# Eight modulation columns moved from the tensor engine to the vector engine, and the softmax's division from the vector engine to the scalar engine

## The chip, the core and the metric

The kernel runs on one core of one Trainium2 chip. A core has engines that run side by side, each through its own list of instructions in order: TensorE (PE in the rows; PEld is its weight load), VectorE (DVE), ScalarE (ACT), GpSimd (POOL) and SyncE (SP), which here issues transfers. The metric is the device time of one execution in microseconds (us), as the median of several runs.

## What is computed

A two-layer backbone of a diffusion generator: 256 latent tokens and 256 context tokens of width 1024. Layer 0 mixes tokens by windowed attention with sink logits and by a two-way gated recurrence (HGRN2), side by side; layer 1 by a two-way retention; each layer ends with a SwiGLU feed-forward. Each sub-layer is modulated by vectors that come from a matrix product of the conditioning with `mod_w`: six chunks of 1024 for each layer (shift, scale and gate, twice), for two streams (latent and context).

```python
m_lat = jnp.split((cond_lat @ mod_w[layer] + mod_b[layer])[:, None, :], 6, axis=-1)
m_ctx = jnp.split((cond_ctx @ mod_w[layer] + mod_b[layer])[None, None, :], 6, axis=-1)
...
s_lat = jnp.where(valid, s_lat, -jnp.inf)
s_ctx = jnp.einsum('bkgqd,bkcd->bkgqc', qb, k_ctx, preferred_element_type=F32) * scale
p = jax.nn.softmax(jnp.concatenate([sink_col, s_lat, s_ctx], axis=-1), axis=-1)
...
x = x + m_lat[2] * y_lat
x = x + m_lat[5] * swiglu(modulate(rms_norm(x, norm_g[layer, 1]), m_lat[3], m_lat[4]), ...)
```

## The kernel before

Activations lie with features on the 128 partitions and tokens along the free axis (latent tokens first, then context). All large products take their weights in fp32 as two parts: `ensure` loads a block of 8 tiles of 128x128 (`raw`), ScalarE rounds it to `whi` (L268), VectorE subtracts to get `wlo` (L269), two blocks ahead of use, and `mm3` (L336 to L338) issues three matmuls for each product. These matmuls set the pace of the program text: `work` counts the columns they stream and calls `tick` every 1600 columns. A tick calls `mod_tick` and then moves one step on in each of several lanes (generators): the attention lane, two HGRN lanes, a lane of norms. The order on each engine is then made by a scheduler that takes priorities from this text; it also sets which instruction of a lane stands before which weight split.

The attention lane works on 24 score blocks of 128 queries (8 heads, 3 blocks each). `softmax_scores` makes a block: two matmuls into a bank of PSUM, on VectorE the maximum (L640, L641), on ScalarE the exponential with its sum (L644) and the sink's term (L646), on VectorE the sum's reciprocal (L647, L648) and the division of the probabilities (L650): one instruction of 512 columns for a latent block, two of 256 columns for a pair of context blocks. Five ticks later `softmax_T` transposes the block on TensorE (L656) and ScalarE copies the result out (L658); `attn_pv` multiplies by the values (L675), and its result is split by L416 and L417. The HGRN lanes have some 30 instructions of VectorE for each of 4 heads (L715 to L816), the lane of norms those of L873 to L880.

The modulation is cut into 80 tasks of 128 output features. Layer 0's chunks 0 and 1 are made ahead of everything by TensorE (`mod0a`, L175). For the rest, `mod_tick` starts tasks at a given number of ticks, in the order of `ORD`, and `mod_until` makes up for those that are missing where a chunk is needed. `mod_load` fetches a task's 128x1024 weights (`mr`, three buffers) up to three tasks ahead. `mod_one` does a task with one multiply-and-sum on VectorE for each stream (L233: an instruction of 1024 columns that leaves its sum in an accumulator, and a read of the accumulator). Chunk 3 of layer 0 (the one in `PES`) goes another way, two tasks at a time, by `mod_pe`: 8 matmuls with the conditioning as the 32-column stationary operand (L206), a copy to SBUF on ScalarE (L209), 2 small matmuls that add up the groups (L212), and a small addition on VectorE (L154). A matmul with plain fp32 operands shows as two records in the trace. Four such pieces stand in the program, and all of chunk 3 falls into the first mixer.

Of the kernel before, what the change touches and what calls it, by code (L numbers as in the profile page):

```python
# [37 lines left out]
FA = 2  # L38
PES = [3]
ORD = [2, 3, 4, 5]  # L40
# [28 lines left out]
def hybrid_kernel(ctx, tc, xT, wst, mw0, mwT, small, cbc, cst, imask, dmat, out, order):  # L69
# [128 lines left out]

    def mod_pe(i):

        l, ch, k = mod_tasks[i]
        ps = axb()
        for j in range(2):
            t = mod_load(i + j)[:].rearrange("p (g n) -> p g n", g=4)
            for g in range(4):
                T.matmul(ps[32 * g:32 * g + 32, 0:L], cT[:, 4 * j + g, :], t[:, g, :], start=(j == 0), stop=(j == 1),  # L206
                         skip_group_check=True)
        part = u()[:, 0:L]
        A.activation(part, ps[:, 0:L], AF.Copy)  # L209
        ps2 = ps[:, L:L + 4].rearrange("p (c s) -> p c s", s=2)  # L210
        for c in range(2):
            T.matmul(ps2[:, c, :], part[:, c * P:(c + 1) * P], sel, start=True, stop=True, skip_group_check=True)  # L212
        mod_finish(l, ch, k, k + 2, ps2.rearrange("p c s -> p s c"))

    def mod_step():
        l, ch, k = mod_tasks[min(mod_pos[0], len(mod_tasks) - 1)]
        return 2 if l == 0 and ch in PES else 1

    def mod_one():
        i = mod_pos[0]  # L220
        n = mod_step()
        mod_pos[0] += n
        if n == 2:
            return mod_pe(i)
        l, ch, k = mod_tasks[i]
        mr = mod_load(i)
        streams = (0, 1) if (l == 0 or ch < 2) else (0,)
        for s in streams:
            if s == streams[-1]:
                o = mr[:]  # L230
            else:
                o = u((P, D), BF16)[:]
            V.tensor_tensor_reduce(o, mr[:], cb[:, s, :], 1.0, 0.0, ALU.mult, ALU.add, mvec(l, s, ch, k))  # L233
        if k == KD - 1:
            mod_finish(l, ch)
# [9 lines left out]
    def mod_tick():  # L245
        tickn[0] += 1
        if tickn[0] >= modt[0] * mod_step():
            tickn[0] -= modt[0] * mod_step()
            if mod_pos[0] < len(mod_tasks):
                mod_one()  # L250
# [368 lines left out]
    def softmax_scores(t, j, which):  # L619
# [29 lines left out]
        for i in range(nq):  # L649
            V.tensor_scalar(p[:, i * w:(i + 1) * w], p[:, i * w:(i + 1) * w], den[:, i:i + 1], None, ALU.mult)  # L650
        return p
# [667 lines left out]
```

## Time and profile before

| | |
|---|---|
| median of 3 runs (lowest to highest) | 1146.19 us (1146.14 to 1147.27) |
| the profiled execution's own time | 1146.45 us |
| its span, first to last instruction | 1144.6 us |
| busy share of the span: TensorE, VectorE, ScalarE | 98%, 67%, 48% |
| share of the span's chain that ended last: TensorE, VectorE, ScalarE, DMA | 84%, 10%, 3%, 1% |

The profiled execution lies 0.26 us above the median; 1.85 us of it lie outside the span. The share of the chain tells which engine's work was the last to end before the next step could start, followed back from the end. A busy share is an average over stages: TensorE's matmuls overlap in the pipeline, so that the engine can read as busy while it loses a few tenths of a microsecond; what it did is better read from when each instruction starts.

### The profile page before, as it was taken

What the parts mean: (1) busy time and instruction counts of PE and PEld (TensorE: products, weight loads), DVE (VectorE), ACT (ScalarE), POOL (GpSimd) and SP (SyncE); (2) the same over time, 40 slices, a digit from 0 to 9 for tenths busy, and PEclk for the clock granted to TensorE, in tenths of its full rate; (3) what the DMA queues carried; (4) which work ended last, traced back from release to release, by engine and by line L of the source; (5) the groups of instructions that cost most, each with busy time, mean ns of one, the idle gap of its engine ahead of it and who ended that gap; (6) DMA issues with size and microseconds to landing.
All of it is one profiled execution on the core that took longest, in us unless ns stands there. A gap on an engine that the chain in (4) does not pass through costs nothing.

```text
span 1144.6 us, 18866 instructions
## 1 busy us (share of the span) xinstructions
PE 1116.4 (98%) x7514; PEld 996.9 (87%) x7514; DVE 767.4 (67%) x1399; ACT 554.0 (48%) x948; POOL 20.8 (2%) x46
## 2 busy tenths in 40 slices
PE   3999999999999999999999998999999999999998
PEld 1777877888998888988888898999999999999998
DVE  3877698899798557357883678374646577555553
ACT  5676676664753231123322476454445657544441
POOL 0012000000000000000000000000000000000000
PEclk9999999999999999999999999999999999999999
DMA  9987221326237446247983324343434265655553
GB/s 329 349 235 184 92 65 66 112 74 202 94 113 241 143 147 202 77 139 237 324 308 109 95 75 129 111 131 109 148 94 147 92 203 167 192 183 181 184 183 109
DMA packets 56121, 182.46 MB, mean 159 GB/s; under 512 B 6368, under 2 KB 9824, under 8 KB 55904
## 3 DMA queue, kind: packets, MB, share of 16 engines
q1 hardware_dynamic: 53648, 176.45, 47.6%
q0 software_dynamic: 2240, 4.72, 1.7%
q8 instruction: 59, 0.97, 0.4%
q14 instruction: 30, 0.25, 0.1%
q10 hardware_dynamic: 144, 0.08, 0.0%
HBM read 177.56 MB, written 1.05 MB: 156 GB/s over the span
## 4 chain that ended last, share of the span: by engine, by line
PE 84%; DVE 10%; ACT 3%; DMA 1%; issue 1%; DVEq 0%; ACTq 0%; SPq 0%
PE mm L338 23%; PE mm L337 23%; PE mm L336 23%; PE ax L337 2%; PE ax L336 2%; PE ax L338 2%; DVE wlo L269 2%; DMA raw<-in_wst_dram 1%; PE ax L175 1%; PE ax L656 1%; ACT whi L268 1%; PE ax L675 1%; DVE u L459 1%; PE mm L411 1%; PE mm L409 1%
## 5 line engine op out<-in xcount | busy, mean ns | idle before, releaser
L268 ACT ACTIVATE whi<-raw 128x1024 fp32r<-128x1024 f32 x230 | 243.3, 1059 | 403.0 <-PE mm L337 242.9
L269 DVE TENSOR_TENSOR wlo<-raw,whi 128x1024 fp32r<-128x1024 f32 x230 | 280.7, 1222 | 166.5 <-ACT whi L268 165.9
L336 PE MATMUL mm<-hh,whi 128*128 128x256 f32 (+1 forms) x1072 | 362.2, 339 | 1.2 <-ACT whi L268 0.9
L338 PE MATMUL mm<-hh,wlo 128*128 128x256 f32 (+1 forms) x1072 | 361.6, 338 | 0.6 <-DVE wlo L269 0.6
L337 PE MATMUL mm<-hl,whi 128*128 128x256 f32 (+1 forms) x1072 | 362.0, 338 | 0.1
L337 PE MATMUL mm<-u,whi 128*128 128x256 f32 (+2 forms) x768 | 236.9, 309 | 0.0
L338 PE MATMUL mm<-u,wlo 128*128 128x256 f32 (+2 forms) x768 | 236.7, 308 | 0.0
L336 PE MATMUL mm<-u,whi 128*128 128x256 f32 (+2 forms) x768 | 236.3, 308 | 0.3 <-DVE x L483 0.3
L338 PEld LDWEIGHTS mm<-hh,wlo 128*128 128x128 f32 x1072 | 204.4, 191 | 21.8 <-DVE wlo L269 0.8
L336 PEld LDWEIGHTS mm<-hh,whi 128*128 128x128 f32 x1072 | 204.2, 191 | 21.9 <-ACT whi L268 0.9
L337 PEld LDWEIGHTS mm<-hl,whi 128*128 128x128 f32 x1072 | 204.3, 191 | 20.2 <-DVE hl L466 0.3
L336 PEld LDWEIGHTS mm<-u,whi 128*128 128x128 f32 x768 | 146.4, 191 | 7.9 <-issue 0.4
L338 PEld LDWEIGHTS mm<-u,wlo 128*128 128x128 f32 x768 | 146.6, 191 | 7.2
L337 PEld LDWEIGHTS mm<-u,whi 128*128 128x128 f32 x768 | 146.6, 191 | 7.1
L233 DVE CUSTOM_DVE_ANT_0 mr<-mr,cb 128x1024 f32<-128x1024 f32 x72 | 87.1, 1222 | 13.2 <-DMA mr<-in_mwT_dram 12.6
L416 ACT ACTIVATE u<-u 128x512 fp32r<-128x512 f32 (+1 forms) x84 | 43.0, 526 | 36.7 <-DVE u L1007 17.3
L1007 DVE TENSOR_TENSOR u<-u,mm 128x512 f32<-128x512 f32 (+1 forms) x40 | 22.1, 553 | 44.7 <-PE mm L338 44.7
L233 DVE CUSTOM_DVE_ANT_0 u<-mr,cb 128x1024 bf16<-128x1024 f32 x40 | 48.4, 1219 | 2.8 <-DMA mr<-in_mwT_dram 1.5
L417 DVE TENSOR_TENSOR u<-u,u 128x512 fp32r<-128x512 f32 (+1 forms) x84 | 46.5, 565 | 5.0 <-ACT u L416 4.9
L336 PE MATMUL ax<-u,u 128*128 128x256 f32 x160 | 45.9, 287 | 3.1 <-ACT u L416 3.1
L483 DVE SCALAR_TENSOR_TENSOR x<-mm,modv,x 128x256 f32<-128x256 f32 x48 | 22.4, 480 | 36.1 <-PE mm L338 36.1
L337 PE MATMUL ax<-u,u 128*128 128x256 f32 x160 | 46.0, 287 | 0.0
(220 smaller groups left out, 1216.4 us busy)
## 6 DMA issues: line engine op xcount, KB each, us to landing
raw<-in_wst_dram SPq DMA_DIRECT2D x230, 512.0 KB, 3.8
mr<-in_mwT_dram SPq DMA_DIRECT2D x80, 512.0 KB, 4.5
u<-in_mw_dram SPq DMA_DIRECT2D x16, 256.0 KB, 5.2
u<-u POOLq DMA_DIRECT2D x20, 128.0 KB, 5.7
u<-in_dmat_dram POOLq DMA_DIRECT2D x8, 256.0 KB, 3.0
raw<-in_mw_dram SPq DMA_DIRECT2D x6, 256.0 KB, 5.2
mr<-in_mw_dram SPq DMA_DIRECT2D x6, 256.0 KB, 5.2
x<-in_xT_dram SPq DMA_DIRECT2D x8, 128.0 KB, 3.4
```

What stands on the lines that cost most here:

```text
L175: T.matmul(ps[32 * g:32 * g + 32, :], cT[:, k, :], mws[nt * 8 + k], start=(k < 4), stop=(k >= 4), skip_group_check=True)
L233: V.tensor_tensor_reduce(o, mr[:], cb[:, s, :], 1.0, 0.0, ALU.mult, ALU.add, mvec(l, s, ch, k))
L268: A.activation(hi[:], src[:], AF.Copy)
L269: V.tensor_tensor(lo[:], src[:], hi[:].bitcast(F32), ALU.subtract)
L336: T.matmul(o, w[0], a[0], start=first, stop=False, skip_group_check=shared)
L337: T.matmul(o, w[0], a[1], start=False, stop=False, skip_group_check=shared)
L338: anchor[0] = T.matmul(o, w[1], a[0], start=False, stop=last, skip_group_check=shared)
L409: T.matmul(ps[t][:], a[0], w[0], start=(k == 0), stop=False)
L416: A.activation(hi, src, AF.Copy)
L417: V.tensor_tensor(lo, src, hi.bitcast(F32), ALU.subtract)
L483: V.scalar_tensor_tensor(xs(m, s), ps[:, sl], mvec(l, s, ch, m), xs(m, s), ALU.mult, ALU.add)
L1007: V.tensor_tensor(g[:, 0:w], g[:, 0:w], ps[2 * i + 1][:, 0:w], ALU.mult)
```

## The change

Chunk 3 of layer 0 is made like all others, and the division in the softmax goes to ScalarE, as a copy with the reciprocal as its scale. `mod_pe` and `mod_step` go; the task counter moves on by one task at each due tick, where a piece of chunk 3 took two tasks at twice the interval. The host lays out the weights of chunk 3 like the rest.

```diff
@@ hybrid_kernel
-    def mod_pe(i):
-
-        l, ch, k = mod_tasks[i]
-        ps = axb()
-        for j in range(2):
-            t = mod_load(i + j)[:].rearrange("p (g n) -> p g n", g=4)
-            for g in range(4):
-                T.matmul(ps[32 * g:32 * g + 32, 0:L], cT[:, 4 * j + g, :], t[:, g, :], start=(j == 0), stop=(j == 1),
-                         skip_group_check=True)
-        part = u()[:, 0:L]
-        A.activation(part, ps[:, 0:L], AF.Copy)
-        ps2 = ps[:, L:L + 4].rearrange("p (c s) -> p c s", s=2)
-        for c in range(2):
-            T.matmul(ps2[:, c, :], part[:, c * P:(c + 1) * P], sel, start=True, stop=True, skip_group_check=True)
-        mod_finish(l, ch, k, k + 2, ps2.rearrange("p c s -> p s c"))
...
     def mod_one():
         i = mod_pos[0]
-        n = mod_step()
-        mod_pos[0] += n
-        if n == 2:
-            return mod_pe(i)
+        mod_pos[0] += 1
         l, ch, k = mod_tasks[i]
...
-        if tickn[0] >= modt[0] * mod_step():
-            tickn[0] -= modt[0] * mod_step()
+        if tickn[0] >= modt[0]:
+            tickn[0] -= modt[0]
...
@@ softmax_scores
         for i in range(nq):
-            V.tensor_scalar(p[:, i * w:(i + 1) * w], p[:, i * w:(i + 1) * w], den[:, i:i + 1], None, ALU.mult)
+            A.activation(p[:, i * w:(i + 1) * w], p[:, i * w:(i + 1) * w], AF.Copy, scale=den[:, i:i + 1])
```

The scheduler makes a new order from this. It differs on TensorE, VectorE, ScalarE and SyncE within layer 0's first mixer alone; from the last heads' norms on, and so through both feed-forwards and all of layer 1, every engine has the same instructions in the same order. Line numbers of the changed kernel are 24 lower behind `mod_pe` (L209 there is the multiply-and-sum, L245 the split, L616 to L626 the softmax, L626 its division).

VectorE, where the attention lane has its first blocks (before, 97.8 to 103.7 us). Before (L593 and L632 prepare queries and scores, L154 ends the first piece of `mod_pe`):

```order
L593 TENSOR_TENSOR u_896<-u_757,u_894 128x512
L632 TENSOR_TENSOR ax_978<-ax_978,u_110 128x128
L640 TENSOR_REDUCE s_982<-ax_978 128x1
L647 TENSOR_TENSOR s_939<-s_939,s_940 128x1
L641 TENSOR_SCALAR s_982<-s_982,nsk 128x1
L648 RECIPROCAL s_939<-s_939 128x1
L650 TENSOR_SCALAR u_943<-u_943,s_939 128x512
L154 TENSOR_TENSOR modv<-ax_960,sml 128x2x2
L269 TENSOR_TENSOR wlo_1065<-raw_1062,whi_1064 128x1024
```

Now, at the same place:

```order
L569 TENSOR_TENSOR u_896<-u_757,u_894 128x512
L608 TENSOR_TENSOR ax_970<-ax_970,u_110 128x128
L209 ISA u_915,modv<-mr_794,cb 128x1024
...
L616 TENSOR_REDUCE s_974<-ax_970 128x1
L209 ISA mr_794,modv<-mr_794,cb 128x1024
...
L623 TENSOR_TENSOR s_944<-s_944,s_945 128x1
L209 ISA u_967,modv<-mr_841,cb 128x1024
...
L624 RECIPROCAL s_944<-s_944 128x1
L617 TENSOR_SCALAR s_974<-s_974,nsk 128x1
L209 ISA mr_841,modv<-mr_841,cb 128x1024
...
L608 TENSOR_TENSOR ax_1028<-ax_1028,u_110 128x128
L245 TENSOR_TENSOR wlo_1057<-raw_1054,whi_1056 128x1024
```

Two tasks stand here, four multiply-and-sums (the reads of the accumulator behind each are left out), between the steps of two softmax blocks and ahead of the split; the division is gone. The other six tasks stand alone, two instructions each: two more before 145 us of the old trace, three between 145 and 205 us, one at some 211 us.

VectorE, where the first HGRN head's second direction begins (before, 150.1 to 153.5 us; L718 is a scan, L720 and L723 use it). Before:

```order
L718 SCALAR_TENSOR_TENSOR u_1520<-u_111,u_1422 128x512
L640 TENSOR_REDUCE s_1548<-ax_1544 128x1
L647 TENSOR_TENSOR s_1507<-s_1507,s_1508 128x2
L720 TENSOR_TENSOR u_1422<-u_1520 128x512
L648 RECIPROCAL s_1507<-s_1507 128x2
L723 TENSOR_TENSOR ex_1523<-u_1520 128x8
L641 TENSOR_SCALAR s_1548<-s_1548,nsk 128x1
L650 TENSOR_SCALAR u_1511<-u_1511,s_1507 128x256 x2
L632 TENSOR_TENSOR ax_1575<-ax_1575,u_110 128x128
L269 TENSOR_TENSOR wlo_1765<-raw_1762,whi_1764 128x1024
```

Now:

```order
L694 SCALAR_TENSOR_TENSOR u_1504<-u_111,u_1406 128x512
L209 ISA u_1523,modv<-mr_1121,cb 128x1024
...
L623 TENSOR_TENSOR s_1491<-s_1491,s_1492 128x2
L696 TENSOR_TENSOR u_1406<-u_1504 128x512
L624 RECIPROCAL s_1491<-s_1491 128x2
L699 TENSOR_TENSOR ex_1507<-u_1504 128x8
L209 ISA mr_1121,modv<-mr_1121,cb 128x1024
...
L616 TENSOR_REDUCE s_1537<-ax_1533 128x1
L608 TENSOR_TENSOR ax_1564<-ax_1564,u_110 128x128
L617 TENSOR_SCALAR s_1537<-s_1537,nsk 128x1
L245 TENSOR_TENSOR wlo_1944<-raw_1941,whi_1943 128x1024
```

One task of two multiply-and-sums stands between the scan and the maximum of the next score block, and the two half divisions are gone.

ScalarE at the same place. Before (L725, L726 and L724 are small exponentials of the HGRN lane, L803 a copy out of PSUM):

```order
L725 ACTIVATE ex_1523<-u_1520 128x8
L726 ACTIVATE ex_1523<-u_1520 128x8
L724 ACTIVATE ex_1523<-ex_1523 128x8
L644 ACTIVATE u_1553,s_1549<-ax_1544,s_1548 128x512
L646 ACTIVATE s_1550<-s_1548,sml 128x1
L658 ACTIVATE u_1573<-ax_1568 128x512
L644 ACTIVATE u_1584,s_1580<-ax_1575,s_1579 128x512
L646 ACTIVATE s_1581<-s_1579,sml 128x1
```

Now:

```order
L701 ACTIVATE ex_1507<-u_1504 128x8
L702 ACTIVATE ex_1507<-u_1504 128x8
L626 ACTIVATE u_1495<-u_1495,s_1491 128x256 x2
L700 ACTIVATE ex_1507<-ex_1507 128x8
L620 ACTIVATE u_1542,s_1538<-ax_1533,s_1537 128x512
L622 ACTIVATE s_1539<-s_1537,sml 128x1
```

The division (L626) stands in ScalarE's list ahead of the next block's exponential, and it waits for the reciprocal (L624) of VectorE's list.

## Rows read from the trace of the kernel before

**Rows 1.** The page's first part: each engine's busy time over the whole span, its share and its number of instructions.

```profile
PE 1116.4 (98%) x7514; PEld 996.9 (87%) x7514; DVE 767.4 (67%) x1399; ACT 554.0 (48%) x948; POOL 20.8 (2%) x46
```

**Rows 2.** The page's second part: busy tenths of TensorE and VectorE in 40 slices of 28.6 us each (slices 4 to 10 hold the first mixer).

```profile
PE   3999999999999999999999998999999999999998
DVE  3877698899798557357883678374646577555553
```

**Rows 3.** The chain that ended last, in order of time, some pieces of it: start in us, length in us, what.

```profile
145.10 0.48 DVE u L650
...
174.55 0.28 ACT u L209
174.87 0.61 PE ax L212 x4
...
232.90 0.68 DVE u L720
...
266.66 1.15 DVE wlo L269
267.87 4.38 DMA raw<-in_wst_dram
```

**Rows 4.** Busy time of each engine in three stretches of the first mixer: stretch, its length, then busy us and (in brackets) instructions of PE, PEld, DVE, ACT and POOL, the granted clock, the share of the DMA engines and GB/s.

```profile
95.00:145.00 50.00, 50.00 (x312) 40.73 (x311) 35.65 (x102) 34.95 (x86) 5.61 (x11) 1.00 0.50 137
145.00:205.00 60.00, 59.36 (x550) 47.36 (x552) 53.77 (x142) 43.60 (x105) 2.28 (x6) 1.00 0.22 72
205.00:277.00 72.00, 71.52 (x564) 59.32 (x556) 68.97 (x142) 42.00 (x90) 1.98 (x5) 1.00 0.37 115
```

**Rows 5.** TensorE in order of time around the first and the third piece of `mod_pe`: start us, us, engine, line, operation, out<-in, shapes, count, and in brackets the idle time before.

```profile
96.13 1.07 PE L206 MATMUL ax<-mr,cT 128*32 128x256 f32 x16
97.13 0.50 PE L626 MATMUL ax<-u,u 128*128 128x512 f32 x1
...
102.79 0.50 PE L212 MATMUL ax<-con,u 128*128 128x2 f32 x4
103.15 0.49 PE L411 MATMUL mm<-whi,hl 128*128 128x512 f32 x1
...
174.04 0.39 PE L336 MATMUL mm<-hh,whi 128*128 128x512 f32 x1
174.87 0.61 PE L212 MATMUL ax<-con,u 128*128 128x2 f32 x4 [0.44 <-ACT u L209]
```

**Rows 6.** Groups of instructions by line and shape, of `mod_pe`'s matmuls on TensorE and its copy on ScalarE: out<-in, shapes, count | busy us, mean ns of one | idle us before them and what ended most of it.

```profile
L206 PE MATMUL ax<-mr,cT 128*32 128x256 f32 x64 | 4.3, 385 | 0.0
L212 PE MATMUL ax<-con,u 128*128 128x2 f32 x16 | 2.2, 243 | 0.4 <-ACT u L209 0.4
L209 ACT ACTIVATE u<-ax 128x256 f32<-128x256 f32 x4 | 1.5, 375 | 1.4 <-PE ax L206 1.4
```

**Rows 7.** VectorE in order of time: two places with the division of the softmax (L650) and the instruction after it, and two multiply-and-sums (L233) in a row.

```profile
145.10 0.48 DVE L650 TENSOR_SCALAR u<-u,s 128x512 f32<-128x512 f32 x1
145.49 1.22 DVE L269 TENSOR_TENSOR wlo<-raw,whi 128x1024 fp32r<-128x1024 f32 x1
...
177.99 0.61 DVE L650 TENSOR_SCALAR u<-u,s 128x256 f32<-128x256 f32 x2
178.52 0.34 DVE L816 SCALAR_TENSOR_TENSOR u<-u,ex,ax 128x128 f32<-128x128 f32 x1
...
264.29 1.22 DVE L233 CUSTOM_DVE_ANT_0 mr<-mr,cb 128x1024 f32<-128x1024 f32 x1
265.44 1.22 DVE L233 CUSTOM_DVE_ANT_0 u<-mr,cb 128x1024 bf16<-128x1024 f32 x1
```

**Rows 8.** The busy time of L650 alone on VectorE in the first two stretches, with the number of instructions.

```profile
95.00:145.00 50.00, 6.79 (x17) 1.00 0.50 137
145.00:205.00 60.00, 5.81 (x15) 1.00 0.22 72
```

**Rows 9.** Groups of instructions on ScalarE by line and shape, as in rows 6: the nearest to a scaled copy in SBUF.

```profile
L416 ACT ACTIVATE u<-u 128x512 fp32r<-128x512 f32 x46 | 29.0, 630 | 36.3 <-DVE u L1007 17.3 <-DVE u L1109 7.8 <-DVE u L880 4.9
L416 ACT ACTIVATE u<-u 128x256 fp32r<-128x256 f32 x38 | 14.0, 401 | 0.5 <-DVE u L1159 0.5
L432 ACT ACTIVATE u<-x,gsv 128x256 fp32r<-128x256 f32 x24 | 11.9, 494 | 0.0
L644 ACT ACTIVATE u<-ax,s 128x512 f32<-128x512 f32 x16 | 11.0, 687 | 7.6 <-DVE s L641 7.3 <-issue 0.3
```

**Rows 10.** What VectorE waited for in the second and in the third stretch, the longest of each: line, released by, us in total, times, longest.

```profile
DVE s L647 <- ACT s L646: 1.8, 2, 1.2
...
DVE u L715 <- ACT u L294: 2.0, 2, 1.5
```

**Rows 11.** Where TensorE starts right behind another engine: ScalarE's copy of transposes and the matmuls after it, and transposes that wait for VectorE.

```profile
149.06 0.58 ACT L658 ACTIVATE u<-ax 128x512 f32<-128x512 f32 x1
...
149.71 0.64 PE L656 MATMUL ax<-con,u 128*128 128x128 f32 x4
...
277.16 0.72 PE L878 MATMUL ax<-con,u 128*128 128x128 f32 x3 [0.43 <-DVE u L873]
```

**Rows 12.** What the multiply-and-sum L233 waited for in the whole run (us, times), and a wait of SyncE's queue of transfers between 90 and 280 us (us in total, times, longest).

```profile
  DMA mr<-in_mwT_dram: 14.0, 17
...
SPq L196 <- PE ax L206: 18.0, 4, 5.0
```

More of the change, by code (lines that the diff above doesn't have):

```diff
@@ L38 @@
 FA = 2
-PES = [3]
 ORD = [2, 3, 4, 5]
@@ L197, in mod_load @@
         return mod_raw[i]
-    def mod_pe(i):
-        l, ch, k = mod_tasks[i]
-        ps = axb()
-        for j in range(2):
-            t = mod_load(i + j)[:].rearrange("p (g n) -> p g n", g=4)
-            for g in range(4):
-                T.matmul(ps[32 * g:32 * g + 32, 0:L], cT[:, 4 * j + g, :], t[:, g, :], start=(j == 0), stop=(j == 1),
-                         skip_group_check=True)
-        part = u()[:, 0:L]
-        A.activation(part, ps[:, 0:L], AF.Copy)
-        ps2 = ps[:, L:L + 4].rearrange("p (c s) -> p c s", s=2)
-        for c in range(2):
-            T.matmul(ps2[:, c, :], part[:, c * P:(c + 1) * P], sel, start=True, stop=True, skip_group_check=True)
-        mod_finish(l, ch, k, k + 2, ps2.rearrange("p c s -> p s c"))
-    def mod_step():
-        l, ch, k = mod_tasks[min(mod_pos[0], len(mod_tasks) - 1)]
-        return 2 if l == 0 and ch in PES else 1
     def mod_one():
         i = mod_pos[0]
-        n = mod_step()
-        mod_pos[0] += n
-        if n == 2:
-            return mod_pe(i)
+        mod_pos[0] += 1
         l, ch, k = mod_tasks[i]
@@ L1270 @@
     for i, ch in enumerate(ORD):
-        cols = slice(ch * D, (ch + 1) * D)
-        if ch in PES:
-            t = mw[0][:, cols].reshape(2, 4, P, 4, 256).transpose(3, 0, 2, 1, 4)
-        else:
-            t = mw[0][:, cols].T
-        mt[8 * i:8 * i + 8] = t.reshape(8, P, D)
+        mt[8 * i:8 * i + 8] = mw[0][:, ch * D:(ch + 1) * D].T.reshape(8, P, D)
     ew = I['even_w_in'][0]
```

## The prediction

> **What bounds the kernel now.** I read the shares first: TensorE is busy 98% of the span, VectorE 67%, ScalarE less than half [rows 1]. An average can hide stages, so the slices come next: TensorE shows 9 nearly everywhere, and VectorE is at 8 or 9 in slices 6 to 11 (143 to 315 us), where the first mixer runs [rows 2]. The change touches only that mixer, so the rest of the span, which is TensorE's, can be set aside.
>
> Inside the mixer I cut three stretches at the places where the chain changes hands: 95 to 145, 145 to 205 and 205 to 277 us. TensorE is busy in all of them (50.00 of 50, 59.36 of 60, 71.52 of 72), at a granted clock of 1.00. VectorE has 35.65 of 50 us in the first, 53.77 of 60 in the second, 68.97 of 72 in the third; ScalarE 34.95, 43.60 and 42.00 [rows 4]. So in the first stretch VectorE has 14.3 us to spare, in the second 6.2, in the third 3.0. The chain says the same in another way: it runs through VectorE from 145.10 us on, with the division itself as its first step, comes back to TensorE at 174.87 us, and is VectorE's again from 232.90 to 267.8 us [rows 3]. The reader should see two engines that are both nearly full: taking work from TensorE helps only as far as VectorE keeps up, and the change loads VectorE.
>
> How close they run is seen where TensorE starts: ScalarE's copy at 149.06 us lasts 0.58 and ends at 149.64; the transposes behind it start at 149.71. At 277.16 us TensorE has waited 0.43 us for VectorE's L873 [rows 11]. There is almost no slack, but hardly any loss either.
>
> **The change, part by part.** *TensorE loses the four pieces.* The 16 records of L206 take 1.00 us from their start to that of the next instruction (96.13 to 97.13), L212 0.36 us (102.79 to 103.15) [rows 5]; by the groups a piece's L212 is busy 2.2/4 = 0.55 us [rows 6]. I take 1.45 us for a piece. The third piece also made TensorE wait: a matmul that is normally followed after 0.23 us was followed after 0.83 (174.04 to 174.87), behind the copy L209 [rows 5], which is 0.60 us more. Two pieces lie in the first stretch, the third in the second; the fourth begins at the border and is counted in the third. Sum: 2.9, 2.05 and 1.45, in all 6.4 us.
>
> *VectorE gains sixteen multiply-and-sums and loses the divisions.* One L233 follows the other after 1.15 us (264.29, 265.44) [rows 7]: 16 x 1.15 = 18.4 us. A division of 512 columns frees the engine after 0.39 us, a pair of 256 after 0.53 [rows 7]. The first stretch holds 17 instructions, which are 9 single ones and 4 pairs, the second 15, which are 7 and 4 pairs [rows 8]: 5.6 and 4.9 us. From the order shown above, eight multiply-and-sums come into the first stretch, six into the second, two into the third. So VectorE's work changes by 9.2 - 5.6 = +3.6 us, 6.9 - 4.9 = +2.0 and +2.3. The three small additions that go with `mod_pe` I put at nothing in sum (some 0.1 us each, against the one larger addition at the end of the chunk).
>
> *ScalarE gains the divisions and loses four copies.* A scaled copy in SBUF with a pointer for the scale is not there at 512 columns. A plain one takes 630 ns, the exponential with pointers 687; at 256 columns a plain one takes 401, a scaled one 494 [rows 9]. Instructions overlap by some 0.1 us on this engine, so that I take 0.6 and 0.4 us; the bounds are 0.5/0.3 and 0.7/0.5. First stretch 9 x 0.6 + 8 x 0.4 = 8.6, second 7.4, less 0.375 for each copy L209 [rows 6]. ScalarE goes to some 42.8 us in the first stretch and 50.6 in the second: of the time that TensorE would leave (47.1 and 57.95) that is 91% and 87%.
>
> VectorE does the same division faster, in 0.39 us to the 0.6 taken here for 512 columns [rows 7, 9]. The Trainium skill (ScalarE: Activation LUTs, Rules for kernel authors) says for multiplications to use VectorE rather than ScalarE. It speaks against this half of the change, and the two rows agree with it in price; the sum by either is the same, since the page prices the instruction and not the queue, but a kernel in which ScalarE then fills up is the second rival below.
>
> *Transfers* cost nothing in the sum: the same 80 loads of modulation weights are issued, three tasks ahead. L233 has waited for them 14.0 us in all, and SyncE has waited 18.0 us for L206 to free buffers [rows 12]; now VectorE frees them. Behind such a load stand weight loads in the same queue. What hides them is the distance of two blocks; if that is used up, a load costs the 4.38 us of [rows 3].
>
> *The new wait.* ScalarE's division waits for VectorE's reciprocal, and behind it on ScalarE stand the next exponential, the copies of transposes and the rounding of weights, for which TensorE and VectorE wait in turn. Before, one engine did reciprocal and division without asking. And each L233 holds VectorE for 1.15 us ahead of a maximum or a reciprocal.
>
> **The sum by stretches.** First: TensorE sets the pace and VectorE's 3.6 us fit into its 14.3. It would be -2.9 us. ScalarE at 91% will cost some of it; I give back 0.6 (bounds: nothing, and all of 2.9): -2.3. Second and third: VectorE's work is 53.77 + 2.0 = 55.8 and 68.97 + 2.3 = 71.3 us, and the stretch lasts that plus what VectorE still idles. It idled 6.2 and 3.0 us, partly for TensorE's pace, partly for ScalarE (L647 for the sink's exponential 1.8 us, L715 for the gates' logarithm 2.0) [rows 10]. The first kind goes when VectorE runs behind, the second stays; bounds are none and all. I take half: 3.1 and 1.5 us. That gives 58.9 and 72.8 us, -1.1 and +0.8. TensorE alone would need 57.95 and 70.55, so VectorE sets both. After 277 us all orders are as before: nothing. Sum: -2.3 - 1.1 + 0.8 = -2.6 us. On the profiled execution's 1146.45 us that is 1143.85, on the median, 0.26 lower, 1143.6.
>
> In one formula, with i for the idle time that is left to VectorE between 145 and 277 us: change = i - 7.2 us. It was 9.2 us, and I take 4.6.
>
> **Rivals.** *TensorE keeps the pace.* If VectorE and ScalarE fill their gaps nearly without loss (i under 2.4), the floor is TensorE's own: -4.8 to -6.4 us, 1139.8 to 1141.4. For it: the scheduler has moved the weight splits ahead of the tasks. Against: VectorE would be at 98% over 130 us in order, with two partners.
>
> *ScalarE takes the pace in the softmax.* Full to 91% on average in the first stretch, it has bursts: if these hold up TensorE's transposes, the first stretch gives back all of its 2.9 us, and the second its 2.05, while the third keeps about its +0.8: 1146 to 1147, no change that counts. For it: TensorE starts 0.07 us behind ScalarE's copies already [rows 11]. Against: five ticks lie between a block's scores and its transposes.
>
> *Slower: VectorE's idle time does not shrink.* Its place is 145 to 277 us, the mechanism the multiply-and-sums that stand in order ahead of what ScalarE and TensorE wait for: VectorE is late with a reciprocal, ScalarE with the division and all behind it, and VectorE then waits for ScalarE's sums (L647) as long as before. With i = 9.2 the second and third stretch are 2.0 and 2.3 us longer; with half of the first stretch's gain given back it is +2.8 us, 1149.0. It decides from i = 7.2 on, that is, if more than three quarters of the old idle time stay.
>
> A result of no effect at all is not among them: the order shows that the instructions move.
>
> **Numbers.** My forecast (VectorE sets the later pace, i between 2.4 and 6): 0.38. TensorE's floor 0.14, ScalarE's pace 0.22, slower 0.26. A measurement of this kernel tells 0.2%, 2.3 us, from no change. Faster by more than that are most of the forecast, all of the floor and a little of ScalarE's case: 0.47. Within it lie the rest of the forecast, most of ScalarE's case and some of the slower one: 0.25. Slower: 0.28. The range 1139.8 to 1149.4 reaches from TensorE's floor to the slower case with its 2.8 us and some 0.4 more; the forecast's own is 1141.2 to 1145.
>
> **What would show it.** The 32-column matmuls between 95 and 211 us are gone and sixteen more multiply-and-sums stand there; VectorE's busy time up by some 8 us in the mixer, ScalarE's by 14 or so. Right: the weight splits of the first stretch come some 2 us earlier than before, VectorE's idle time in the two later stretches is about half, and from the feed-forward on everything is ahead by the same 2 to 3 us. Wrong, if TensorE shows waits for ScalarE between 100 and 145 us (then the 0.6 was too small), if the divisions take over 0.7 us, or if VectorE's idle time stays near 9 us; or if a weight block lands late behind a modulation load.

## The result

The changed kernel takes 1155.03 us (median; 1153.80 to 1155.58), the kernel before, timed beside it, 1146.73 (1146.14 to 1147.48): a ratio of 1.0071 with a 95% interval of 1.0053 to 1.0088. It is slower by 8.3 us, where 2.6 us less was forecast, and lies 5.6 us above the range. One execution of run p2 below and one of the kernel before beside e9 to e11 took far longer (1233.43 and 1372.35 us, at a granted clock of 0.85 and 0.76) and are left out of the ratios.

The page of the changed kernel: its span, its busy shares, the slices of VectorE and the chain's shares, to be held against [rows 1, 2].

```profile
span 1152.0 us, 18746 instructions
...
PE 1115.5 (97%) x7434; PEld 994.4 (86%) x7434; DVE 772.0 (67%) x1396; ACT 568.0 (49%) x976; POOL 20.6 (2%) x46
...
DVE  3978689899889567347884568463746577555553
...
PE 86%; DVE 9%; ACT 3%; issue 1%; DMA 1%; DVEq 0%; ACTq 0%
```

The shares hardly move. The three stretches of [rows 4], their borders shifted to about the same places of VectorE's list (columns as there):

```profile
95.00:145.00 50.00, 50.00 (x284) 41.34 (x283) 36.13 (x94) 41.50 (x98) 5.35 (x11) 1.00 0.49 136
145.00:211.00 66.00, 60.50 (x559) 48.48 (x558) 57.32 (x146) 53.34 (x124) 2.89 (x8) 1.00 0.26 81
211.00:285.00 74.00, 70.31 (x506) 55.76 (x504) 69.84 (x146) 41.10 (x88) 1.16 (x4) 1.00 0.32 102
```

TensorE, which missed 0.64 and 0.48 us of the last two stretches before, now misses 5.5 and 3.7 us. VectorE has more work and still idles 8.7 and 4.2 us.

To place the loss I use a mark that all kernels have: L888 (L864 in the changed kernel), the gate of the recurrence, eight instructions on VectorE. Each needs a large product and ScalarE's tanh of it; behind the last one only the mixer's end is left. The row of that line in the kernel before and in the changed kernel (count, shortest/median/longest ns, start of the first and the last), and the stretches ahead of the first and between the two:

```profile
L888 DVE SCALAR_TENSOR_TENSOR u<-u,mm x8: 676/684/690, 137.5 to 260.3; 128x512 f32<-128x512 f32 x8
95.00:137.50 42.50, 42.50 (x271) 34.45 (x270) 29.31 (x85) 27.70 (x70) 5.61 (x11) 1.00 0.57 152
137.50:260.30 122.80, 121.95 (x1078) 99.66 (x1077) 113.01 (x274) 86.81 (x195) 4.27 (x11) 1.00 0.24 77
```

```profile
L864 DVE SCALAR_TENSOR_TENSOR u<-u,mm x8: 676/683/689, 138.3 to 269.4; 128x512 f32<-128x512 f32 x8
95.00:138.30 43.30, 43.30 (x249) 35.74 (x248) 31.87 (x85) 34.83 (x84) 5.35 (x11) 1.00 0.56 157
138.30:269.40 131.10, 125.41 (x1045) 100.72 (x1044) 117.32 (x272) 93.89 (x209) 4.05 (x11) 1.00 0.25 77
```

The first gate comes 0.8 us late, the last one 9.1. From the last gate to the end of the span it is 1144.6 - 260.3 = 884.3 us before and 882.6 now. So the loss arises between the gates (8.3 us, with 0.8 ahead of them and 1.7 won back behind, which makes the 7.4 between the two spans): VectorE's work grew from 113.0 to 117.3 us, its idle time from 9.8 to 13.8.

What VectorE waited for there in the changed kernel, the longest (line, released by, us in total, times, longest):

```profile
DVE u L864 <- ACT u L863: 4.5, 3, 2.9
DVE u L691 <- ACT u L270: 3.7, 2, 2.4
DVE u L393 <- ACT u L392: 2.3, 2, 1.6
DVE u L709 <- ACT u L708: 1.3, 2, 1.0
DVE s L623 <- ACT s L622: 0.9, 1, 0.9
```

All are waits for ScalarE (1.47 us of the first line belong to the first gate itself and lie just ahead of the stretch). One of them in order of time (start us, us, engine, line):

```profile
169.06 1.28 ACT L890 ACT_TABLE_LOAD   x1
...
169.41 0.16 DVE L624 RECIPROCAL s<-s 128x1 f32<-128x1 f32 x1
169.48 0.20 DVE L617 TENSOR_SCALAR s<-s,nsk 128x1 f32<-128x1 f32 x1
...
170.35 0.60 ACT L890 ACTIVATE u<-mm 128x512 f32<-128x512 f32 x1
170.85 0.71 ACT L626 ACTIVATE u<-u,s 128x512 f32<-128x512 f32 x1
...
171.46 0.59 ACT L890 ACTIVATE u<-mm 128x512 f32<-128x512 f32 x1
...
171.94 0.60 ACT L863 ACTIVATE u<-mm 128x512 f32<-128x512 f32 x1
...
172.57 0.69 DVE L864 SCALAR_TENSOR_TENSOR u<-u,mm 128x512 f32<-128x512 f32 x1 [2.89 <-ACT u L863]
```

VectorE is through at 169.68, and the gate is next in its list; ScalarE loads a table, goes through what stands in its queue, the division L626 among it, and only then makes the tanh (L863) that the gate waits for.

### The profile page after: what moved, and what is told of

Same layout as the page of the kernel before. It is cut to its first block, busy times and chain, and to the rows that moved or that the text cites. A ratio compares the mean times of both kernels' runs of the same rounds, so it can differ in the third digit from the quotient of the medians.

```text
span 1152.0 us, 18746 instructions
## 1 busy us (share of the span) xinstructions
PE 1115.5 (97%) x7434; PEld 994.4 (86%) x7434; DVE 772.0 (67%) x1396; ACT 568.0 (49%) x976; POOL 20.6 (2%) x46
## 4 chain that ended last, share of the span: by engine, by line
PE 86%; DVE 9%; ACT 3%; issue 1%; DMA 1%; DVEq 0%; ACTq 0%
PE mm L312 24%; PE mm L314 24%; PE mm L313 24%; PE ax L313 3%; PE ax L312 3%; PE ax L314 3%; DVE wlo L245 2%; PE ax L174 1%; DVE u L209 1%; DVE mr L209 1%; DMA mr<-in_mwT_dram 1%; DVE u L720 1%; PE mm L385 1%; PE mm L386 1%; PE mm L387 1%
## 5 line engine op out<-in xcount | busy, mean ns | idle before, releaser
L245 DVE TENSOR_TENSOR wlo<-raw,whi 128x1024 fp32r<-128x1024 f32 x230 | 280.6, 1222 | 167.1 <-ACT whi L244 166.3
L209 DVE CUSTOM_DVE_ANT_0 mr<-mr,cb 128x1024 f32<-128x1024 f32 x80 | 96.9, 1221 | 14.4 <-DMA mr<-in_mwT_dram 13.6
L209 DVE CUSTOM_DVE_ANT_0 u<-mr,cb 128x1024 bf16<-128x1024 f32 x48 | 58.1, 1217 | 1.6 <-ACT cb L500 1.2
L393 DVE TENSOR_TENSOR u<-u,u 128x512 fp32r<-128x512 f32 (+1 forms) x84 | 46.4, 564 | 5.0 <-ACT u L392 5.0
```

The source lines that it names most:

```text
L245: V.tensor_tensor(lo[:], src[:], hi[:].bitcast(F32), ALU.subtract)
L393: V.tensor_tensor(lo, src, hi.bitcast(F32), ALU.subtract)
```

## The experiments

### Which half of the change

Theory A blamed the division on ScalarE, theory B VectorE's load, theory C the new order on TensorE. The traces show the shift that C means: when TensorE comes to the 408th record of its large matmuls (L336 to L338), it has shown 794 other records in the kernel before (at 197.9 us) and 550 in the changed kernel (at 185.6 us). The large ones are pulled ahead.

e1: the changed kernel with the division on VectorE.

```diff
-            A.activation(p[:, i * w:(i + 1) * w], p[:, i * w:(i + 1) * w], AF.Copy, scale=den[:, i:i + 1])
+            V.tensor_scalar(p[:, i * w:(i + 1) * w], p[:, i * w:(i + 1) * w], den[:, i:i + 1], None, ALU.mult)
```

> All chunks by multiply-and-sum, the division stays on VectorE. Theory A (the division on ScalarE makes a ring: VectorE's reciprocal, ScalarE's division and what stands behind it, VectorE's next step): without it the loss goes, 1143 to 1147 us, and TensorE's stalls behind ScalarE between 145 and 211 us (about 6 us in the changed kernel) go too. Theory B (sixteen multiply-and-sums, 18.4 us, are too much for VectorE): VectorE now has 10.5 us more work than in the changed kernel, so that it is slower still, 1156 to 1165 us. Theory C (the order: in the changed kernel the large matmuls stand much earlier among those of attention and HGRN, and TensorE then has none left to fill with; the order here has the same shift): about as the changed kernel, 1151 to 1156 us, with stalls at the same places.

Measured: 1154.81 us (1154.45 to 1155.75), ratio 1.0069 [1.0055, 1.0083].

e2: the reverse edit on the kernel before.

> The kernel before with the division alone moved to ScalarE; chunk 3 stays on TensorE. Theory A: the ring is here whole, 1151 to 1156 us, against 1146.7 before. Theory B: VectorE is freed of 10.5 us and has no more to do, so the time falls, 1138 to 1144 us. Theory C: the shift of the large matmuls on TensorE is here only in the second half of the mixer, so about a third to a half of the loss, 1148 to 1151 us.

Measured: 1147.84 us (1146.43 to 1149.65), ratio 1.0007 [0.9998, 1.0016]: no difference that this measurement tells.

e3: the changed kernel without the division.

```diff
-        for i in range(nq):
-            A.activation(p[:, i * w:(i + 1) * w], p[:, i * w:(i + 1) * w], AF.Copy, scale=den[:, i:i + 1])
```

> The changed kernel with the softmax's division left out altogether (the probabilities stay undivided), so that neither VectorE nor ScalarE has it; the order of the large matmuls is still shifted. Theory A: the ring is cut and both engines are lighter, 1140 to 1145 us. Theory B: VectorE's load is that of the changed kernel, 1152 to 1156 us. Theory C: the same shift, 1150 to 1155 us.

Measured: 1150.54 us (1149.25 to 1151.76), ratio 1.0029 [1.0017, 1.0040].

e4: the kernel before with `V.tensor_scalar` of the division as `G.tensor_scalar`.

> The kernel before with the division moved to GpSimd, which is busy 2% of the span; chunk 3 stays on TensorE, and TensorE's order is nearly that of before. It takes 10.5 us from VectorE and gives ScalarE nothing. Theory A: no ring through ScalarE, so a gain, as far as VectorE sets the end: 1139 to 1145 us. Theory B: the same, 1138 to 1144 us. Theory C: no shift, no loss, and little gain, 1144 to 1147 us. If a division on GpSimd takes several us, or slows VectorE's instructions beside it, it is 1147 us or more in all three.

Measured: 1147.67 us (1146.72 to 1148.53), ratio 1.0004 [0.9996, 1.0013].

The loss goes with the multiply-and-sums: e1 has all of it. Theory A is out as its cause. In the whole time the division's place is worth nothing that can be seen: in e2 and e4 VectorE loses 5.6 and 3.4 us of work between the gates and idles 4.1 and 3.8 us more. Left out altogether (e3), the division gives 4.5 us back. The first of e2's two rows is the stretch between its gates, to be held against 113.01 of 122.80 above; the second one of its waits:

```profile
139.50:260.80 121.30, 120.52 (x1070) 98.88 (x1069) 107.43 (x256) 93.48 (x210) 4.05 (x11) 1.00 0.24 75
...
DVE u L715 <- ACT u L294: 3.5, 2, 1.9
```

VectorE idles 13.9 us there instead of 9.8. But TensorE is busy in 120.52 of the 121.30 us, so e2 does not tell what VectorE's relief is worth where VectorE sets the pace. B and C are not told apart by these runs. Against B, VectorE is busy 10.7 us more in e1 than in the changed kernel (782.7 and 772.0 us) at the same time, and e2 and e3 fell 3.8 above and 1.5 us below its ranges. C had e1 and e3; e2 and e4 came 0.2 us below and 0.7 above its ranges.

### Load, order or place

e5: the changed kernel with chunk 3's sums over 128 columns; e6: the same with the division on VectorE.

```diff
-            V.tensor_tensor_reduce(o, mr[:], cb[:, s, :], 1.0, 0.0, ALU.mult, ALU.add, mvec(l, s, ch, k))
+            w = P if l == 0 and ch == 3 else D
+            V.tensor_tensor_reduce(o[:, 0:w], mr[:, 0:w], cb[:, s, 0:w], 1.0, 0.0, ALU.mult, ALU.add, mvec(l, s, ch, k))
```

> The changed kernel with chunk 3's sixteen multiply-and-sums over the first 128 of 1024 columns only, so that the chunk is not the reference's: the same instructions and loads, but some 16 us less of VectorE's time. The large matmuls are shifted on TensorE nearly as in the changed kernel. Load theory (VectorE is full between 137 and 282 us of the mixer with a part of its idle time that stays whatever it has to do, so each us of work there is a us of the end): most of the loss goes and a part of TensorE's freed 6.4 us shows, 1141 to 1146 us. Order theory (the shift itself makes TensorE run out of work): 1149 to 1154 us.

Measured: 1147.94 us (1145.56 to 1149.81), ratio 1.0003 [0.9994, 1.0012].

> Chunk 3's multiply-and-sums over 128 columns as in the run before, and the division on VectorE; TensorE's order is then nearly that of the kernel before. Against the kernel before TensorE loses its 6.4 us and VectorE gains some 3 us. Load theory: VectorE's end sets it, 1146 to 1149 us, or down to 1143 where the first 40 us of the mixer pass on TensorE's gain. Order theory: no shift, TensorE's gain is kept, 1140 to 1143 us.

Measured: 1142.15 us (1140.26 to 1144.14), ratio 0.9958 [0.9946, 0.9970].

Shortening the sums gives back 7.1 us (the changed kernel to e5) and 12.7 us (e1 to e6). In e6 the scheduler's order changed as well: by the 408th large record TensorE has shown 734 others there, against 550 in e1. e6 came inside the range of the order theory and just under that of the load theory; it shows 4.8 us of TensorE's gain. e5 fell between the ranges of the two theories, but it is the run that separates them: it has 550 others at that mark, as the changed kernel has, and little of the loss, so the shift alone is not the cause. Of the 3.7 us between the profiled executions of e5 and e6, 0.8 lie ahead of the first gate, 2.3 between the gates and 0.6 behind (the table below). Behind the gates, TensorE has run out of large matmuls. Busy time of TensorE, granted clock, DMA share and GB/s there, of e5:

```profile
270.00:275.00 5.00, 3.04 (x14) 1.00 0.77 263
275.00:280.00 5.00, 4.05 (x12) 0.51 0.75 249
280.00:285.00 5.00, 5.00 (x20) 0.81 0.64 214
```

and of e6:

```profile
270.00:275.00 5.00, 4.62 (x22) 1.00 0.89 297
275.00:280.00 5.00, 4.72 (x22) 1.00 0.54 166
280.00:285.00 5.00, 5.00 (x24) 1.00 0.53 170
```

In e5 TensorE stood 2.91 us for ScalarE's L393, and the granted clock was then 0.51, the lower level (1.2 of 2.4 GHz), which costs on top of the wait. Why the medians of e5 and e6 are 5.8 us apart, and the profiled executions 3.7, stays open.

e7: the changed kernel with tasks started sooner; e8: e7 with the division on GpSimd.

```diff
-MODT = [4.6, 5.5, 4, 4]
+MODT = [2.0, 5.5, 4, 4]
...
-            if mod_pos[0] < len(mod_tasks):
+            if mod_pos[0] < (24 if modt[0] == MODT[0] else len(mod_tasks)):
```

> The changed kernel with the tasks of chunks 3 and 4 started every 2.0 ticks of the mixer in place of 4.6, up to the 24 tasks that the feed-forward needs: three more tasks (6.9 us of VectorE) come before the first head's split, into the stretch in which VectorE still idles 11 us, and no burst of five is left at the end. The shift of the large matmuls stays. Load theory: 5 to 7 us less between 138 and 282 us, 1147 to 1151 us. Order theory: 1153 to 1156 us. If the tasks in the first stretch hold up the softmax there, 1154 to 1158 us.

Measured: 1161.69 us (1160.15 to 1162.01), ratio 1.0125 [1.0111, 1.0139].

> As the run before, with the division on GpSimd in place of ScalarE (an instruction took 1.59 us there at 512 columns and 1.22 at 256 in the run of the kernel before with the division on GpSimd). Load theory: neither VectorE nor ScalarE has the division, some 2 to 4 us better than the run before it, 1143 to 1148 us. If the longer way from the reciprocal over GpSimd to the transposes costs as much as ScalarE's queue, the same as the run before. Order theory: 1153 to 1156 us.

Measured: 1157.64 us (1157.36 to 1158.43), ratio 1.0093 [1.0079, 1.0107].

All cases missed e7. It put 14 sums ahead of the first gate in place of 8, and 18 between the gates in place of 14; the first gate came at 144.6 us. So neither "VectorE's whole load" nor "room in the first stretch" without a limit is right. e8 is 4.1 us better than e7, the upper end of what taking the division from ScalarE was to give.

e9 (on e1), e10 (on the changed kernel) and e11 (on the kernel before): weight splits of the mixer to GpSimd.

```diff
-            V.tensor_tensor(lo[:], src[:], hi[:].bitcast(F32), ALU.subtract)
+            E = G if modt[0] == MODT[0] else V
+            E.tensor_tensor(lo[:], src[:], hi[:].bitcast(F32), ALU.subtract)
```

> All chunks by multiply-and-sum, the division on VectorE (as in e1, 1154.8 us), and the sixteen weight splits wlo of the first mixer from the recurrence's start on go from VectorE to GpSimd (sixteen by 1.22 us, 19.5 us less for VectorE, and work that is made two blocks ahead of its use). Load theory (VectorE's sums cost time because VectorE is full in the mixer): VectorE has about the work of the kernel before, and TensorE's 6.4 us show: 1141 to 1146 us. If it was not the load (the order, or the sums as such): 1151 to 1156 us. If a split takes so long on GpSimd (over 4 us), or slows VectorE's instructions beside it, that TensorE waits for weights: 1150 us or more with waits of TensorE for wlo.

> The changed kernel with the same sixteen splits on GpSimd; VectorE then has some 12 us less than in the kernel before, the division stays on ScalarE. Load theory: 1141 to 1146 us, and VectorE idle by 10 us more. If the way over ScalarE (reciprocal, division, transposes) sets the pace whatever VectorE has to do: 1148 to 1153 us.

> The control: the kernel before with the same sixteen splits on GpSimd. TensorE has its whole work and stalls only some 1.5 us there, so VectorE's relief can give little: 1144 to 1147 us. Where GpSimd's splits hold up TensorE or slow VectorE it is 1148 us or more, and then the two runs above have that loss in them too.

Measured: 1172.05, 1174.22 and 1164.67 us; ratios 1.0216 [1.0203, 1.0230], 1.0235 [1.0221, 1.0250], 1.0157 [1.0143, 1.0170]. The control itself lost 17.6 us, so the other two say nothing on load; they lie 7.4 and 9.6 us above it, about the change's loss once more. Why the control lost is in the last section.

p1: the kernel before with half of chunk 3 on VectorE (the host's layout follows).

```diff
-        return 2 if l == 0 and ch in PES else 1
+        return 2 if l == 0 and ch in PES and k < 4 else 1
```

> The kernel before with half of chunk 3 changed: its first four tasks stay two pieces on TensorE, the other four become eight multiply-and-sums on VectorE (9.2 us); the division stays on VectorE. If every sum costs from the first on (load of the lanes' time): half of e1's loss, 1150 to 1152 us. If VectorE has room for some, and the loss begins only when it is full: 1145 to 1148 us.

Measured: 1155.71 us (1155.01 to 1157.63), ratio 1.0072 [1.0060, 1.0085]: as much as all of chunk 3, and above both ranges.

p2: the edit of e7 on the kernel before. p3 and p4: the changed kernel with 7 and 10 for 4.6 in `MODT`.

> The kernel before with its modulation tasks started every 2.0 ticks of the mixer in place of 4.6, up to the 24 that the feed-forward needs: the sums of chunk 4, most of which stand in a burst behind the lanes' last split, then stand among the softmax and recurrence. No instruction is added or taken away. Lanes theory (a sum costs while the lanes run, and is covered by TensorE's remaining matmuls behind them): 1152 to 1157 us. Load theory (only the sum of VectorE's work counts): 1145 to 1149 us.

Measured: 1157.04 us (1156.26 to 1158.24), ratio 1.0082 [1.0068, 1.0095].

> The changed kernel with the tasks started every 7 ticks in place of 4.6: some four tasks (9.2 us) fewer stand among the lanes, and the burst behind them is longer by as many. Lanes theory: the lanes end 4 to 7 us earlier; as the longer burst may in turn hold up the last norms, 1148 to 1153 us. Load theory: 1154 to 1156 us.

> As p3 with every 10 ticks: only three or four tasks stand among the lanes after the first two, the burst is ten tasks or so (23 us). Lanes theory: the lanes end 8 to 10 us earlier than in the changed kernel, but TensorE's remaining matmuls no longer cover the burst: 1150 to 1158 us, with TensorE's stalls all behind the last split. Load theory: 1154 to 1156 us.

Measured: 1158.07 and 1161.33 us, ratios 1.0094 [1.0081, 1.0108] and 1.0127 [1.0111, 1.0142]. In p2 no work was added, and ten sums moved ahead of the last gate cost some 9 us. In p3 and p4 the last gate came 4.7 and 7.4 us earlier than in the changed kernel, about as the lanes theory had it, but the burst behind it then held up TensorE, and both times lie above all their ranges. p4's wait behind the last gate:

```profile
PE mm L313 <- DVE u L393: 7.8, 1, 7.8
```

q1 is the mirror of p1, q2 a quarter of it, q3 q1 with the first piece of chunk 4 on TensorE as well.

```diff
-PES = [3]
+PES = [(3, 2), (3, 3)]              # q1
+PES = [(3, 1), (3, 2), (3, 3)]      # q2
+PES = [(3, 2), (3, 3), (4, 0)]      # q3
...
-        return 2 if l == 0 and ch in PES else 1
+        return 2 if l == 0 and (ch, k // 2) in PES else 1
```

> The mirror of p1: the first four tasks of chunk 3, which fall into 98 to 130 us, become eight multiply-and-sums on VectorE, the last four stay two pieces on TensorE (169 and 205 us in the kernel before); the division stays on VectorE. Place theory (VectorE sets the pace from 137 to 270 us alone; before it TensorE does, and VectorE has 13 us to spare there): TensorE's 2.9 us are kept, 1143 to 1145.5 us. If any change of the order costs, or a sum costs wherever the lanes run: 1149 to 1156 us.

Measured: 1144.44 us (1141.84 to 1144.88), ratio 0.9973 [0.9962, 0.9985].

> Only the first two tasks of chunk 3 (98 to 103 us) as multiply-and-sums, the other six as three pieces on TensorE. TensorE's order is the same as before but for the first few large matmuls. Place theory: half of the gain of q1, 1145 to 1146.5 us. If a sum costs wherever the lanes run: 1148 to 1151 us.

Measured: 1146.01 us (1143.22 to 1147.26), ratio 0.9990 [0.9981, 0.9999].

> q1, and in addition the first two tasks of chunk 4 (four multiply-and-sums at 223 to 244 us in the kernel before) as a piece on TensorE: VectorE loses 4.6 us where it sets the pace, TensorE gains 1.45 us. Place theory: the lanes end 2 to 4 us earlier than in q1, and as TensorE's own work is 1.45 us more, the time is 1141 to 1145 us. If TensorE alone sets the end: 1.5 us more than q1.

Measured: 1145.51 us (1144.86 to 1146.67), ratio 0.9986 [0.9978, 0.9995]: 0.5 us above the place theory's range, and 1.1 above q1.

The place decides. The stretches of p1 and then of q1, ahead of the first gate and between the gates:

```profile
95.00:136.80 41.80, 41.80 (x268) 33.91 (x267) 28.65 (x85) 27.58 (x70) 4.36 (x9) 1.00 0.56 152
136.80:269.20 132.40, 128.74 (x1064) 103.49 (x1063) 123.13 (x289) 86.09 (x192) 4.59 (x12) 1.00 0.25 79
```

```profile
95.00:135.80 40.80, 40.80 (x241) 34.18 (x240) 36.91 (x101) 26.89 (x68) 5.78 (x12) 1.00 0.61 168
135.80:257.80 122.00, 120.79 (x1068) 98.65 (x1067) 112.11 (x273) 86.83 (x195) 4.07 (x11) 1.00 0.24 75
```

Eight sums ahead of the first gate raise VectorE's work there from 29.3 to 36.9 us and its idle time falls from 13.2 to 3.9, while TensorE, busy all the time, is done 1.7 us sooner. Eight sums between the gates raise VectorE's work by 10.1 us and the stretch by 9.6; the idle time stays at 9.3. The same marks in all runs that tell of it (sums: multiply-and-sums after 95 us; work and idle are VectorE's between the gates; end: from the last gate to the span's end):

```
kernel   sums ahead, between | first gate, last | between = work + idle | end   | median
before          0    6       | 137.5   260.3    | 122.8   113.0    9.8 | 884.3 | 1146.7
after           8   14       | 138.3   269.4    | 131.1   117.3   13.8 | 882.6 | 1155.0
e1              8   14       | 134.9   267.4    | 132.5   120.9   11.6 | 885.4 | 1154.8
e2              0    6       | 139.5   260.8    | 121.3   107.4   13.9 | 885.3 | 1147.8
e3              8   14       | 134.0   265.0    | 131.0   118.2   12.8 | 883.8 | 1150.5
e4              0    6       | 138.1   261.3    | 123.2   109.6   13.6 | 885.0 | 1147.7
e5 (short)      -    6       | 135.9   260.2    | 124.3   108.0   16.3 | 885.8 | 1147.9
e6 (short)      -    6       | 135.1   257.1    | 122.0   114.0    8.0 | 885.2 | 1142.2
e7             14   18       | 144.6   275.9    | 131.3   119.5   11.8 | 884.3 | 1161.7
e8             14   18       | 140.8   271.6    | 130.8   121.2    9.6 | 884.0 | 1157.6
p1              0   14       | 136.8   269.2    | 132.4   123.1    9.3 | 886.7 | 1155.7
p2              0   16       | 139.1   270.8    | 131.7   123.7    8.0 | 884.4 | 1157.0
p3              6   10       | 137.9   264.7    | 126.8   112.0   14.8 | 891.0 | 1158.1
p4              6    7       | 138.3   262.0    | 123.7   108.5   15.2 | 897.6 | 1161.3
q1              8    6       | 135.8   257.8    | 122.0   112.1    9.9 | 884.2 | 1144.4
q2              4    6       | 135.4   258.0    | 122.6   112.8    9.8 | 886.2 | 1146.0
q3              8    2       | 136.4   258.6    | 122.2   109.3   12.9 | 886.0 | 1145.5
```

The end is nearly the same everywhere but in p3 and p4, so the last gate gives the time. With six full sums or fewer between the gates the stretch is 121 to 124 us, TensorE's own pace (121.95 of 122.8 us busy before); with 14 or more it is VectorE's work plus 8 to 14 us, 131 to 132.5. q3 took four more sums out of it and gained nothing there: TensorE sets the pace already. q1 is the version that beats both kernels, by 2.6 us and 10.6 us. TensorE's order shifts along with the sums in most of these runs: the others ahead of the 408th large record are 794 before, 687 in q1, 630 in p2, 590 in p1 and 550 in e1. e5, with 550, bounds what the shift may cost between the gates by 2.3 us (124.3 to e6's 122.0), with the division's place in it.

## Why the prediction was wrong

*The step that failed* is "I take half: 3.1 and 1.5 us" of VectorE's idle time, the i of the formula. It was taken for room of which half would be used. In the prediction's own stretches i came out at 12.8 us (66.00 - 57.32 and 74.00 - 69.84), where 4.6 was taken and 9.2 was the bound. With 12.8 the formula gives +5.6, and +7.9 without the 2.3 us that were forecast for the first stretch and did not come; the spans differ by 7.4. Between the gates the idle time went from 9.8 to 13.8 us. With the division on VectorE it stayed at 8 to 12 us whatever work was added (p1 9.3 with 10.1 us more work, p2 8.0 with 10.7, e1 11.6 with 7.9): so it was not spare capacity. The waits are hand-offs, mostly from ScalarE; the longest of p1:

```profile
DVE u L888 <- ACT u L887: 1.7, 1, 1.7
DVE u L733 <- ACT u L732: 1.5, 2, 1.2
DVE s L647 <- ACT s L646: 1.4, 2, 1.1
DVE u L715 <- ACT u L294: 1.3, 1, 1.3
```

In the kernel before they could be mistaken for room, since TensorE set the pace there. By estimate from the table it stood where the two meet: 113.0 us of work and some 9 of waits make 122, and with less work for VectorE the stretch stayed at 121 to 123 (e2, e4, q3).

*VectorE's work* was right: +2.0 and +2.3 us forecast behind 145 us, +4.3 found between the gates. But the sum set the divisions that leave (4.9 us) against the sums that come (9.2) as if they weighed the same. They don't. Eight sums cost the stretch nearly one to one (p1: 10.1 us of work, 9.6 of stretch). Taking the divisions from VectorE where it sets the pace (e1 to the changed kernel) took away 3.6 us of its work and shortened the stretch by 1.4; VectorE idles 2.2 us more, with ScalarE's queue holding the divisions, as at 170.85 us above.

*The first stretch*: "TensorE sets the pace and VectorE's 3.6 us fit" was right for the sums: q1 kept 2.6 us of TensorE's 2.9, e1's first gate came 2.6 us early. With the division on ScalarE too, the gate came 0.8 us late, 3.4 later than in e1. The prediction gave back 0.6 us here for ScalarE, with 2.9 as the bound: a second term that was too small. The gate waits for its tanh (L863), which stands behind a pair of divisions in ScalarE's list; before and in e1 VectorE went on to this gate without a wait. The rows of the changed kernel:

```profile
136.36 0.91 ACT L626 ACTIVATE u<-u,s 128x256 f32<-128x256 f32 x2
...
137.18 0.58 ACT L890 ACTIVATE u<-mm 128x512 f32<-128x512 f32 x1
...
137.66 0.58 ACT L863 ACTIVATE u<-mm 128x512 f32<-128x512 f32 x1
...
138.27 0.69 DVE L864 SCALAR_TENSOR_TENSOR u<-u,mm 128x512 f32<-128x512 f32 x1 [1.47 <-ACT u L863]
```

TensorE shows no wait up to this gate, so the sign that the prediction had named, waits of TensorE for ScalarE between 100 and 145 us, did not show. In e2, whose gate was 2.0 us late, the gate did not wait itself; an instruction ahead of it (L632) waited 1.66 us for a score matmul. How the rest of that delay comes about stays open.

*TensorE's loss of 6.4 us* was real for the most part: e6 shows 4.8 of it where the sums take an eighth of their columns.

*ScalarE's price* was right. The two shapes on ScalarE (busy us, mean ns, idle before):

```profile
L626 ACT ACTIVATE u<-u,s 128x512 f32<-128x512 f32 x16 | 11.5, 719 | 3.0 <-DVE s L624 1.7 <-DVE ex L699 1.0
L626 ACT ACTIVATE u<-u,s 128x256 f32<-128x256 f32 x16 | 7.3, 505 | 3.2 <-DVE s L624 1.6 <-DVE ex L699 1.5
```

These are durations, 0.72 and 0.51 us; the prediction's 0.6 and 0.4 leave out the overlap with the next instruction. From its start to the next one's, a division of 512 columns took 0.61 us (170.85 to 171.46) and a pair of 256 took 0.82 (136.36 to 137.18). ScalarE's total of 14 us more came out too (568.0 against 554.0). By its duration the larger shape is past the sign "over 0.7 us", which so told nothing. The Trainium skill (Perfetto Trace Analysis, Optimizing Scalar/DVE Operations) says that offloading to ScalarE may make sense if VectorE is saturated. Here it was nearly full between the gates in e1 (120.9 of 132.5 us), and the offload, e1 to the changed kernel, gave nothing in the whole time (1154.8 to 1155.0).

*The rivals.* "Slower: VectorE's idle time does not shrink" named the place and the kind of mechanism, but not the hand-off: VectorE's wait for ScalarE's sums fell from 1.8 to 0.9 us between the gates, and the waits for the gates' tanh grew from 0.8 to 3.0, without the first gate's own. Its 1149.0 was too low. Against the profiled execution's 1153.80 us (1149.25 on that footing) 4.0 us are idle time that grew, which none of the cases allowed, and 2.2 the first stretch (+0.8 where it had -1.45), less the 1.7 gained behind the last gate. "ScalarE takes the pace" had the first stretch right, which gave back its whole gain, though by VectorE's gate and not by TensorE's transposes; it is not the cause of the loss, since e1 loses as much without ScalarE's divisions.

*Transfers* show no cost, as said. The waits of the multiply-and-sums for their loads are 13.6 us in the whole run against 14.0 in [rows 12], and in the burst at the end VectorE goes from one to the next:

```profile
277.75 1.22 DVE L209 CUSTOM_DVE_ANT_0 u<-mr,cb 128x1024 bf16<-128x1024 f32 x1
...
279.10 1.22 DVE L209 CUSTOM_DVE_ANT_0 u<-mr,cb 128x1024 bf16<-128x1024 f32 x1
...
280.25 1.22 DVE L209 CUSTOM_DVE_ANT_0 mr<-mr,cb 128x1024 f32<-128x1024 f32 x1
...
281.80 1.20 PE L312 MATMUL mm<-u,whi 128*128 128x512 f32 x4 [2.23 <-ACT u L392]
```

The wait of TensorE in the last row looks like a loss; but from the last gate on the changed kernel is 1.7 us shorter. That TensorE had done part of these matmuls ahead fits the shift of the large matmuls; no run tests it. "After 277 us as before" held in the same sense.

*One reading* was off, without effect: VectorE's slices from 143 to 315 us read 9, 8, 8, 9, 9 and 7 [rows 2], not 8 or 9 throughout.

## To carry to other kernels

Before counting an engine's idle time as room, ask which engine sets the pace of that stretch: beside a partner that is full, idle time may be hand-offs that stay when work is added, and then each microsecond of work is one of the end. Price an edit by the stretch that each instruction falls into: half of this one was a gain of 2.6 us and the other half a loss of 8 us or more. Work that leaves an engine gives little back if the partner that takes it then answers later: 1.4 of 3.6 us here, and the start of the stretch lost more than that.

## What the runs showed of the hardware

*GpSimd's splits hold up VectorE.* In e11 (its lines are one or two higher) a weight split takes 2.4 us on GpSimd, twice VectorE's 1.22. Beside it an addition of one column on VectorE, 153 ns in the mean before, waits it out:

```profile
173.00 2.38 POOL L270 TENSOR_TENSOR wlo<-raw,whi 128x1024 fp32r<-128x1024 f32 x1 [13.26 <-ACT whi L268]
...
173.48 0.68 DVE L641 TENSOR_REDUCE s<-ax 128x1 f32<-128x512 f32 x1
...
174.08 1.32 DVE L648 TENSOR_TENSOR s<-s,s 128x1 f32<-128x1 f32 x1
```

It ends at 175.40, the split at 175.38; the reduction beside it took its usual 0.68 us. VectorE's additions of that line went from 153 to 522 ns in the mean. Others grew too, some with one input in SBUF (L716, a scaling of 512 columns, from 541 to 788 ns). VectorE's instructions of the mixer grew by some 24 us in sum (an estimate from the means of each group in both traces), where the sixteen splits had freed 19.5. This goes far to explain the control's loss; that it is all of it is not shown. The Trainium skill (SBUF — State Buffer, SBUF: two separate sides) tells of an exclusive lock that GpSimd shares with VectorE's instructions of two SBUF inputs, held for the whole instruction. The rows of the addition and the reduction agree.

*After one wait of TensorE the clock fell, after another it did not.* In e5 TensorE stood 2.91 us, and the clock granted over the next five was 0.51, with the matmuls of 512 columns at 0.43 us from one to the next instead of 0.23. In the changed kernel a wait of 2.23 us at 281.80 was followed at 1.00.
